# Sample keys and values as one transfer per chunk, Toeplitz matrix and state-space output as one transfer each, U loads and tap stores issued by GpSimd

## The chip, the cores and the metric

The kernel runs on one core of a Trainium2 chip. The metric is the device time of one execution in microseconds. The core has five engines with an instruction stream each: PE (TensorE, matrix products), DVE (VectorE), ACT (ScalarE), POOL (GpSimd) and SP (SyncE), and DMA engines that move data between the chip's memory and the core. A transfer is issued by SP, ACT or POOL and lands later.

## The reference

One inference step of a decoder layer, for a prompt of 1024 tokens and, with the same weights, a sample group of 8 sequences with 4 new tokens each. The mixer runs a dilated attention (8 heads) beside a diagonal state-space model (32 groups of 16 channels, 64 complex states):

```python
q, k, v, u = jnp.split(x @ w_in, [D_ATT, 2 * D_ATT, 3 * D_ATT], axis=-1)
o_att = attend(q, k, v).reshape(Bn, L, D_ATT)
y_ssm, h_re, h_im = s5_mixer(u, h0_re, h0_im, ...)
mixed = jnp.concatenate([rms_norm(o_att, g_att), rms_norm(y_ssm, g_ssm)], axis=-1) @ w_out
x = layer_norm(DEEPNORM_ALPHA * x + mixed, ln1_g, ln1_b)
x = layer_norm(DEEPNORM_ALPHA * x + memory_attention(x, ...), ln2_g, ln2_b)
x = layer_norm(DEEPNORM_ALPHA * x + (jax.nn.silu(x @ w_gate) * (x @ w_up)) @ w_down, ln3_g, ln3_b)

# in s5_mixer, per group: h_t = abar h_(t-1) + bbar u_t, then
y = Re(C h) + D u;  g = gelu(y);  out = g * sigmoid(g @ w_glu + b_glu)
# sample attention: keys and values are [cache of 1024 rows | 4 new rows] of each sequence
```

## The kernel before

The work of interest lies in the first fifth of the execution, in the projection, the state-space part and the sample attention, which are written as interleaved generators.

**Projection.** PE multiplies the weights (split in two parts, `whi` and `wlo`) with the inputs (`a0h`, `a0l`, ...). Lines 209 to 211 give U, the queries and the keys; lines 427 to 429, in gemm_v, give the values. The weights come as `wraw`, loaded by ACT (L180) and split by ACT (L190) and DVE (L191).

**Sample attention.** The eight sequences form two groups (gr) of four batches, and the 1024 cached rows of a sequence form chunks c. For each group and chunk, `load` (L703 to L707) fetches keys ("ckT") or values ("cv") of four batches into tiles called skv. `scores` (L712) multiplies keys with queries; DVE and ACT form the softmax; L772 multiplies the probabilities with the values, chunk by chunk and batch by batch into four strips of one result, L778 adds the new rows, which a small load (L776) puts in a buffer of the same kind, and DVE reads the result in L780. Keys are used while U, queries and keys are projected, values while the values are projected.

**State space.** It runs in two halves (qf) of 16 groups. DVE and POOL build the matrices Bs and CA (L1426 to L1428), U is loaded from `s_u` (L1433), PE transposes Bs (L1437) and ACT copies it into ET (L1439). L1448 forms the taps kp, which are stored to `s_kp` (L1454) and loaded back as a Toeplitz matrix M (L1471). L1466 makes the inputs of the states, HX, DVE and POOL run the chain of steps over them (L1479 to L1500), L1510 and L1514 form Y, and ACT applies the gelu (L1517). The final states go out in L1519, as runs of nine numbers. Y, which lies in a buffer shared with Bs, goes to `s_y` (L1522).

**GLU.** `glu` loads `s_y` back as gT (L494), ACT and DVE split it (L508, L509), and PE multiplies it with weights, between the parts of the prompt's attention (from L594 on), which loads Q, K, Vn and Vf (L564 to L571) on SP.

**Order.** The code says what depends on what; a scheduler then writes each engine's instruction list. Within an engine, instructions start in this order, and an issue that waits holds up all issues behind it. [...]

Of the kernel before, what the change touches and what calls it, by code (L numbers as in the profile page):

```python
# [140 lines left out]
class Body:  # L141
# [121 lines left out]
    def phase12(self, st):  # L263
        tc, nc, a = self.tc, self.nc, self.a
        A = [self.unit("a0"), self.unit("a1")]
        xa = lambda b, k: (A[k // 4][b][0][:, k % 4, :], A[k // 4][b][1][:, k % 4, :])
        scr = lambda name, shape: self.dp.tile(shape, F32, name=name, tag=name)
        self.s_u = scr("s_u", [512, 8 * 144])
        self.s_y = scr("s_y", [512, 8 * 136])
        self.s_kp = scr("s_kp", [2, 16, 16, 240])  # L270
        self.s_q = scr("s_q", [512, 1024])
        self.s_k = scr("s_k", [512, T])
        self.s_v = scr("s_v", [T, 512])
        self.s_mk = scr("s_mk", [128, 2048])
        self.s_mv = scr("s_mv", [128, 2048])
        self.s_z = scr("s_z", [128, 8 * T])
        self.s_x1 = scr("s_x1", [128, 8 * T])
        self.s_h = {(f, b): scr(f"s_h{f}_{b}", [128, 2 * BLK[b][1]]) for f in range(NF // 2) for b in range(3)}
        self.qs = self.t(self.cp, [128, 4, 32], "qs")
        self.ks = self.t(self.cp, [128, 4, 32], "ks")  # L280
        self.os = self.t(self.cp, [128, 4, 32], "os")
        self.qsum = self.t(self.cp, [128, 32], "qsum")
        with tc.tile_pool(name="ostage", bufs=1) as og:
            self.project(A, xa, og)
        self.rest()
# [202 lines left out]
    def glu(self):  # L488
        tc, nc, a = self.tc, self.nc, self.a
        with tc.tile_pool(name="glu", bufs=1) as gp:  # L490
            G, self.mix1 = self.unit("a0"), self.unit("a1")
            gT = self.t(gp, [128, 4, 8, 136], "gT")
            for n in range(4):
                nc.sync.dma_start(gT[:, n].rearrange("p t c -> p (t c)"), self.s_y[n * 128:(n + 1) * 128, :])  # L494
            src = []
# [200 lines left out]
    def sample_attn(self, ap):  # L696
# [6 lines left out]
        def load(src, gr, c):  # L703
            t_ = [self.t(ap, [128, 512], "skv", bufs=8) for _ in range(4)]
            for b4 in range(4):
                nc.sync.dma_start(t_[b4][:], a[src][4 * gr + b4, c])
            return t_  # L707

# [31 lines left out]
    def sample_finish(self, ap, probs, load, scores, masked, tsel, bsel):  # L740
# [15 lines left out]
        for gr, (S, nm, qb) in enumerate(probs):  # L756
# [12 lines left out]
            for c in range(5):  # L769
                vt = load("cv", gr, c)  # L770
                for b4 in range(4):
                    mm(po[32 * b4:32 * b4 + 32, :], PT[:, 128 * c + 32 * b4:128 * c + 32 * b4 + 32], vt[b4][:],  # L772
                       start=c == 0, stop=False)
                yield
            vs = self.t(ap, [128, 512], "skv", bufs=8)
            nc.sync.dma_start(vs[:32], self.s_v[1024:1056, :])  # L776
# [558 lines left out]
    def ssm(self):  # L1335
# [73 lines left out]
        for qf in range(2):  # L1409
# [22 lines left out]
            for i in range(8):  # L1432
                nc.sync.dma_start(U[16 * i:16 * i + 16], su[:, 16 * qf:16 * qf + 16, 7 - i, :])  # L1433
            for q in range(4):
# [18 lines left out]
            for j in range(4):  # L1453
                nc.sync.dma_start(self.s_kp[qf].rearrange("h (q j) x -> h q j x", j=4)[:, :, j, :],  # L1454
                                  kp[32 * j:32 * j + 16].rearrange("p q n h -> p q (n h)"))
# [13 lines left out]
            M = H("ET", (128, 16, 128))  # L1469
            for i in range(8):  # L1470
                g.dma_start(M[16 * i:16 * i + 16], self.s_kp[qf, :, :, 16 * i:16 * i + 128])  # L1471
            X = HX[:, :, :, 9:137].rearrange("p g r (J j) -> p g r J j", j=8)
# [46 lines left out]
            g.dma_start(a["st"][:, gs], HX[:, :, :, 136:145])  # L1519
            sy = self.s_y[:].rearrange("(g h) (t c) -> h g t c", h=16, t=8)  # L1520
            for t_ in range(8):
                nc.sync.dma_start(sy[:, 16 * qf:16 * qf + 16, t_, :], Y[16 * t_:16 * t_ + 16])  # L1522

# [15 lines left out]
```

## Time and profile before

| | |
|---|---|
| median of 3 runs | 1690.15 us (1688.38 to 1690.17) |
| profiled execution | 1694.87 us |
| its span, first to last instruction | 1693.1 us |
| mean granted clock of PE in it | 0.974 |
| busy: PE, DVE, ACT, POOL | 95%, 55%, 35%, 33% |
| bytes moved | 200.71 MB, mean 119 GB/s |

The span is the time from the first to the last instruction, all times in rows are counted from its start. The profiled execution is one more run, taken with the profiler, so its time differs from the median of the others. The granted clock is the share of the full 2.4 GHz that PE got; 0.50 is 1.2 GHz. PEld is PE's loading of weights, which overlaps with its products.

### The profile page before, as it was taken

How to read it: one execution, taken by the hardware profiler on the slowest of the kernel's cores; microseconds unless marked ns; L12 is line 12 of the kernel's file. 1: busy time of each engine (PE TensorE's matmuls, PEld its weight loads, DVE VectorE, ACT ScalarE, POOL GpSimd, SP SyncE). 2: the span in 40 equal slices, each digit the busy share in tenths (PEclk: the TensorE clock that was granted, in tenths of full speed). 3: DMA queues.
4: the chain of work that ended last, by engine and by line, in shares of the span. 5: the costliest groups of instructions: out<-in, count | busy, mean ns of one | idle time of the engine just before them, and what ended most of it. 6: DMA issues, size and time to landing. Idle time of an engine off the chain costs nothing.

```text
span 1693.1 us, 27820 instructions
## 1 busy us (share of the span) xinstructions
PE 1607.1 (95%) x10910; PEld 1468.4 (87%) x10910; DVE 932.8 (55%) x1785; ACT 598.8 (35%) x1164; POOL 558.6 (33%) x568
## 2 busy tenths in 40 slices
PE   7999899899999988999999999999999999999996
PEld 7997765676776977987798989999999999999995
DVE  7655555266544986235537776555555545545545
ACT  5221221266334155235514444333333333211212
POOL 3433413042223545002126555444444441000134
PEclk9998999989999999999999999999999999999998
DMA  7547967613422356226630222222222224422301
GB/s 276 133 101 193 247 169 179 218 61 107 138 74 84 123 193 226 69 75 207 230 115 26 94 70 76 76 76 76 76 76 77 79 77 147 134 76 69 116 38 65
DMA packets 97683, 200.71 MB, mean 119 GB/s; under 512 B 10384, under 2 KB 52880, under 8 KB 96784
## 3 DMA queue, kind: packets, MB, share of 16 engines
q1 hardware_dynamic: 73456, 137.43, 26.0%
q10 hardware_dynamic: 23232, 59.26, 10.8%
q0 software_dynamic: 864, 2.25, 0.9%
q8 instruction: 86, 1.41, 0.3%
q14 instruction: 45, 0.37, 0.1%
HBM read 153.85 MB, written 45.04 MB: 117 GB/s over the span
## 4 chain that ended last, share of the span: by engine, by line
PE 79%; DMA 7%; DVE 6%; issue 2%; ACT 2%; POOL 2%; SPq 1%; POOLq 0%; ACTq 0%; DVEq 0%
PE g L1051 16%; PE g L209 13%; PE g L211 13%; PE g L210 13%; PE s L1051 7%; PE s L594 2%; PE s L596 2%; DMA skv<-in_cv_dram 1%; DMA wraw<-in_wst_dram 1%; PE g L618 1%; DMA skv<-in_ckT_dram 1%; POOL z L855 1%; DVE wlo L191 1%; PE q L772 1%; DMA hr<-s_h 1%
## 5 line engine op out<-in xcount | busy, mean ns | idle before, releaser
L209 PE MATMUL g<-a0h,whi 128*128 128x384 f32 (+1 forms) x768 | 255.4, 334 | 12.6 <-ACT whi L190 9.4
L211 PE MATMUL g<-a0h,wlo 128*128 128x384 f32 (+1 forms) x768 | 251.8, 328 | 3.5 <-DVE wlo L191 3.5
L210 PE MATMUL g<-a0l,whi 128*128 128x384 f32 (+1 forms) x768 | 252.6, 329 | 0.5 <-DVE a0l L509 0.5
L210 PE MATMUL g<-a1l,whi 128*128 128x384 f32 (+1 forms) x672 | 217.7, 324 | 3.8 <-DVE a1l L337 1.8
L209 PE MATMUL g<-a1h,whi 128*128 128x384 f32 (+1 forms) x672 | 220.2, 328 | 0.8 <-ACT a1h L335 0.8
L211 PE MATMUL g<-a1h,wlo 128*128 128x384 f32 (+1 forms) x672 | 217.6, 324 | 0.0
L209 PEld LDWEIGHTS g<-a0h,whi 128*128 128x128 f32 x768 | 147.9, 193 | 19.8 <-ACT whi L190 9.6
L190 ACT CAST whi<-wraw 128x1024 fp32r<-128x1024 f32 x84 | 88.0, 1050 | 186.9 <-PE g L210 103.1
L211 PEld LDWEIGHTS g<-a0h,wlo 128*128 128x128 f32 x768 | 148.0, 193 | 4.8 <-DVE wlo L191 4.3
L210 PEld LDWEIGHTS g<-a0l,whi 128*128 128x128 f32 x768 | 147.9, 193 | 2.0 <-DVE a0l L509 0.7
L191 DVE TENSOR_TENSOR wlo<-wraw,whi 128x1024 fp32r<-128x1024 f32 x84 | 115.7, 1380 | 47.5 <-ACT whi L190 47.3
L209 PEld LDWEIGHTS g<-a1h,whi 128*128 128x128 f32 x672 | 127.5, 190 | 5.7 <-issue 2.8
L210 PEld LDWEIGHTS g<-a1l,whi 128*128 128x128 f32 x672 | 127.4, 190 | 5.2 <-DVE a1l L337 2.0
L211 PEld LDWEIGHTS g<-a1h,wlo 128*128 128x128 f32 x672 | 127.4, 190 | 0.4 <-issue 0.2
L1044 DVE TENSOR_TENSOR wlo<-wt,wlo 128x512 fp32r<-128x512 f32 x100 | 91.9, 920 | 26.2 <-ACT wlo L1043 24.3
L1043 ACT CAST wlo<-wt 128x512 fp32r<-128x512 f32 x100 | 62.0, 620 | 113.3 <-PE g L1051 91.7
L800 DVE TENSOR_TENSOR z<-z,g 128x384 f32<-128x384 f32 (+1 forms) x96 | 49.1, 518 | 88.5 <-PE g L211 88.3
L808 POOL TENSOR_TENSOR acc<-z 128x384 f32<-128x384 f32 (+1 forms) x6 | 8.5, 1416 | 187.3 <-DVE z L800 173.5
L606 POOL TENSOR_SCALAR S<-S,rD 128x128 f32<-128x128 f32 (+7 forms) x64 | 38.4, 607 | 87.7 <-DVE rD L605 54.1
L855 POOL TENSOR_SCALAR z<-z,vneg,vecs 128x384 f32<-128x384 f32 (+1 forms) x36 | 50.5, 1414 | 43.6 <-DVE z L851 43.6
L1219 POOL TENSOR_SCALAR S<-S,rD 128x256 f32<-128x256 f32 x32 | 15.2, 478 | 113.3 <-DVE rD L1208 105.7
L594 PE MATMUL s<-K,Q 64*128 64x256 f32 (+1 forms) x128 | 42.2, 438 | 5.1 <-DVE nm L602 5.1
(459 smaller groups left out, 4031.1 us busy)
## 6 DMA issues: line engine op xcount, KB each, us to landing
wraw<-in_wst_dram ACTq DMA_DIRECT2D x88, 512.0 KB, 4.0
skv<-in_ckT_dram SPq DMA_DIRECT2D x40, 256.0 KB, 5.0
skv<-in_cv_dram SPq DMA_DIRECT2D x40, 256.0 KB, 4.5
wraw<-in_wst_dram SPq DMA_DIRECT2D x20, 512.0 KB, 4.4
wru<-in_wst_dram SPq DMA_DIRECT2D x20, 512.0 KB, 4.2
hr<-s_h SPq DMA_DIRECT2D x22, 384.0 KB, 3.4
kvm<-in_cmk_dram SPq DMA_DIRECT2D x16, 512.0 KB, 4.9
wraw<-in_cmv_dram SPq DMA_DIRECT2D x16, 512.0 KB, 4.3
```

What stands on the lines that cost most here:

```text
L190: self.nc.scalar.copy(h[:], r[:])
L191: self.nc.vector.tensor_tensor(out=l[:], in0=r[:], in1=h[:], op=OP.subtract)
L209: mm(out, wh, xh, start=start, stop=False)
L210: mm(out, wh, xl, start=False, stop=False)
L211: mm(out, wl, xh, start=False, stop=stop)
L594: mm(ps[:, 32 * nf:w], q, k[:, 128 * max(qt - 1, 0):128 * qt + 128], start=True, stop=True)
L606: g.tensor_scalar(out=S[:, :w], in0=S[:, :w], scalar1=rD[:], scalar2=1.0, op0=OP.mult, op1=OP.mult)
L800: self.nc.vector.tensor_tensor(out=z[:, k], in0=z[:, k], in1=ps[:, :n], op=OP.add)
L855: g.tensor_scalar(out=z[:, k], in0=z[:, k], scalar1=sc, scalar2=bi, op0=OP.mult, op1=OP.add)
L1043: act.copy(t_[:, 0], src)
L1044: v.tensor_tensor(out=t_[:, 1], in0=src, in1=t_[:, 0], op=OP.subtract)
L1051: nc.tensor.matmul(ps[:, :n], p_, q_, start=first and k + j == 0, stop=k == 3 and j == 2, skip_group_check=not first)
```

## The change

Four things change. (1) `load` fetches the four batches of a chunk by one transfer of 1 MB into one tile, of which there are two, instead of four transfers of 256 KB into four of eight tiles; eighty issues become twenty. (2) The U loads (8 for each half) and the tap stores (4 for each half) are issued by POOL instead of SP. (3) The Toeplitz matrix of a half is loaded by one transfer, still from POOL, instead of eight. (4) Y is stored by one transfer for each half instead of eight, to an `s_y` whose layout has the half, h, group and t on axes of their own; the four gT loads read from it with an outer dimension of 8. The runs that the transfers consist of keep their lengths. Line numbers shift by at most one: L1471 becomes L1472, L1519 becomes L1520 and L1522 becomes L1521.

```diff
@@ -266,7 +266,7 @@
         xa = lambda b, k: (A[k // 4][b][0][:, k % 4, :], A[k // 4][b][1][:, k % 4, :])
         scr = lambda name, shape: self.dp.tile(shape, F32, name=name, tag=name)
         self.s_u = scr("s_u", [512, 8 * 144])
-        self.s_y = scr("s_y", [512, 8 * 136])
+        self.s_y = scr("s_y", [2, 16, 16, 8 * 136])
         self.s_kp = scr("s_kp", [2, 16, 16, 240])
         self.s_q = scr("s_q", [512, 1024])
         self.s_k = scr("s_k", [512, T])
@@ -491,7 +491,8 @@
             G, self.mix1 = self.unit("a0"), self.unit("a1")
             gT = self.t(gp, [128, 4, 8, 136], "gT")
             for n in range(4):
-                nc.sync.dma_start(gT[:, n].rearrange("p t c -> p (t c)"), self.s_y[n * 128:(n + 1) * 128, :])
+                nc.sync.dma_start(gT[:, n],
+                                  self.s_y[n // 2, :, 8 * (n % 2):8 * (n % 2) + 8, :].rearrange("h g x -> g h x"))
             src = []
             for b in range(3):
                 off, w = BLK[b]
@@ -701,10 +702,9 @@
             nc.sync.dma_start(d[:], s)
 
         def load(src, gr, c):
-            t_ = [self.t(ap, [128, 512], "skv", bufs=8) for _ in range(4)]
-            for b4 in range(4):
-                nc.sync.dma_start(t_[b4][:], a[src][4 * gr + b4, c])
-            return t_
+            t_ = self.t(ap, [128, 4, 512], "skv", bufs=2)
+            nc.sync.dma_start(t_[:], a[src][4 * gr:4 * gr + 4, c].rearrange("b p n -> p b n"))
+            return [t_[:, b4] for b4 in range(4)]
 
         def scores(o, n, q, keys):
             for hp in range(4):
@@ -769,10 +769,10 @@
             for c in range(5):
                 vt = load("cv", gr, c)
                 for b4 in range(4):
-                    mm(po[32 * b4:32 * b4 + 32, :], PT[:, 128 * c + 32 * b4:128 * c + 32 * b4 + 32], vt[b4][:],
+                    mm(po[32 * b4:32 * b4 + 32, :], PT[:, 128 * c + 32 * b4:128 * c + 32 * b4 + 32], vt[b4],
                        start=c == 0, stop=False)
                 yield
-            vs = self.t(ap, [128, 512], "skv", bufs=8)
+            vs = self.t(ap, [128, 512], "skv", bufs=2)
             nc.sync.dma_start(vs[:32], self.s_v[1024:1056, :])
             for b4 in range(4):
                 mm(po[32 * b4:32 * b4 + 32, :], PT[:32, 640 + 32 * b4:672 + 32 * b4], vs[:32], start=False, stop=True)
@@ -1430,7 +1430,7 @@
             ET, U = H("ET", (128, 8, 2, 128)), H("U", (128, 16, 144))
             su = self.s_u[:].rearrange("(g h) (s c) -> h g s c", h=16, s=8)
             for i in range(8):
-                nc.sync.dma_start(U[16 * i:16 * i + 16], su[:, 16 * qf:16 * qf + 16, 7 - i, :])
+                g.dma_start(U[16 * i:16 * i + 16], su[:, 16 * qf:16 * qf + 16, 7 - i, :])
             for q in range(4):
                 ps = self.ps2()
                 for j in range(4):
@@ -1451,7 +1451,7 @@
             act.copy(kp[:, :, 7:15, :].rearrange("p q n h -> p q (n h)"), ps[:, :512].rearrange("p (q x) -> p q x", q=4))
             v.tensor_tensor(out=kp[:, :, 7, :], in0=kp[:, :, 7, :], in1=dd[:, 4 * qf:4 * qf + 4, :], op=OP.add)
             for j in range(4):
-                nc.sync.dma_start(self.s_kp[qf].rearrange("h (q j) x -> h q j x", j=4)[:, :, j, :],
+                g.dma_start(self.s_kp[qf].rearrange("h (q j) x -> h q j x", j=4)[:, :, j, :],
                                   kp[32 * j:32 * j + 16].rearrange("p q n h -> p q (n h)"))
             yield
 
@@ -1467,8 +1467,9 @@
                            U[:, 2 * gl + z, 8:144], start=True, stop=True)
                 act.copy(HX[:, gl, :, 9:145], ps[:, 0:272].rearrange("p (r c) -> p r c", r=2))
             M = H("ET", (128, 16, 128))
-            for i in range(8):
-                g.dma_start(M[16 * i:16 * i + 16], self.s_kp[qf, :, :, 16 * i:16 * i + 128])
+            taps = self.s_kp[qf]
+            taps = bass.AP(taps.tensor, taps.offset, [[16, 8], *[list(x) for x in taps.ap[:2]], [1, 128]])
+            g.dma_start(M[:], taps)
             X = HX[:, :, :, 9:137].rearrange("p g r (J j) -> p g r J j", j=8)
             qa = lambda e_: e_[:, gs].unsqueeze(2)
             m1, m2 = S("w1", (128, 8, 2, 16)), S("w2", (128, 8, 2, 16))
@@ -1517,9 +1518,7 @@
                     act.activation(Y[:].rearrange("p (g z) c -> p z g c", z=2)[:, z, g0:g0 + cnt, :],
                                    pz[z][:, :136 * cnt].rearrange("p (g c) -> p g c", c=136), AF.Gelu_apprx_tanh)
             g.dma_start(a["st"][:, gs], HX[:, :, :, 136:145])
-            sy = self.s_y[:].rearrange("(g h) (t c) -> h g t c", h=16, t=8)
-            for t_ in range(8):
-                nc.sync.dma_start(sy[:, 16 * qf:16 * qf + 16, t_, :], Y[16 * t_:16 * t_ + 16])
+            nc.sync.dma_start(self.s_y[qf].rearrange("h g (t c) -> t (h g) c", t=8), Y[:])
 
 
 
```

First the order on SP, around the store of the first half's Y. Before, the key tile of chunk 2 of the second group (skv_2069 is its last) is followed by U loads, the eight s_y stores and then chunk 3, whose first tile is skv_2126:

```order
L706 DMA skv_2069<-in_ckT_dram 128x512
L1433 DMA U_2214<-s_u 16x16x144 x3
L1522 DMA s_y<-Bs_1775 16x16x136 x8
L1433 DMA U_2214<-s_u 16x16x144
L706 DMA skv_2126<-in_ckT_dram 128x512
```

In the changed kernel the same place reads as follows; skv_1956 to skv_2120 are chunks 1 to 4 of the second group, and skv_2646 is the first value chunk:

```order
L706 DMA skv_1956<-in_ckT_dram 128x4x512
L706 DMA skv_2010<-in_ckT_dram 128x4x512
L1521 DMA s_y<-Bs_1738 8x256x136
L706 DMA skv_2064<-in_ckT_dram 128x4x512
L706 DMA skv_2120<-in_ckT_dram 128x4x512
L706 DMA skv_2646<-in_cv_dram 128x4x512
```

The U loads have left SP; the store of Y still stands between chunks 2 and 3, as one issue. On SP behind the second half's Y, before and then after:

```order
L1522 DMA s_y<-Bs_3052 16x16x136 x8
L494 DMA gT_3445<-s_y 128x1088 x2
L558 DMA mask_3175<-in_mask_p_dram 128x448
L564 DMA Q_3177<-s_q 128x1024
L564 DMA K_3178<-s_k 128x1024
L569 DMA Vn_3425<-s_v 128x8x128
L571 DMA Vf_3426<-s_v 128x4x128 x2
L494 DMA gT_3445<-s_y 128x1088 x2
```

```order
L1521 DMA s_y<-Bs_2917 8x256x136
L494 DMA gT_3297<-s_y 128x1x1088 x2
L559 DMA mask_3027<-in_mask_p_dram 128x448
L565 DMA Q_3029<-s_q 128x1024
L565 DMA K_3030<-s_k 128x1024
L570 DMA Vn_3277<-s_v 128x8x128
L572 DMA Vf_3278<-s_v 128x4x128 x2
L494 DMA gT_3297<-s_y 128x1x1088 x2
```

One issue of s_y stands there instead of eight, and all that follows keeps its order. On PE, the value products (L772) of chunk 2 of the first group stand as follows before; skv_2809 to skv_2812 are the four batches, and L427 to L429 belong to the projection of the values:

```order
L429 MATMUL g_2780<-whi_2120,a1l_15_84 128x256
L772 MATMUL q_2726<-skv_2809,qb_2714 32x512
L772 MATMUL q_2726<-skv_2810,qb_2714 32x512
L427 MATMUL g_2821<-whi_2060,a0h_8_77 128x256
L428 MATMUL g_2821<-wlo_2061,a0h_8_77 128x256
L429 MATMUL g_2821<-whi_2060,a0l_9_78 128x256
L427 MATMUL g_2821<-whi_2060,a0h_8_77 128x256
L428 MATMUL g_2821<-wlo_2061,a0h_8_77 128x256
L772 MATMUL q_2726<-skv_2811,qb_2714 32x512
L429 MATMUL g_2821<-whi_2060,a0l_9_78 128x256
L427 MATMUL g_2821<-whi_2060,a0h_8_77 128x256
L428 MATMUL g_2821<-wlo_2061,a0h_8_77 128x256
```

The third batch stands five projection matmuls behind the second, the fourth comes five further on. The batches of chunks 3 and 4 of that group and of chunks 2 and 3 of the other stand apart in the same way. In the changed kernel, all four batches of every chunk stand together, here those of chunk 2 (skv_2716), as one row with x4:

```order
L427 MATMUL g_2722<-whi_2004,a0h_8_77 128x256
L428 MATMUL g_2722<-wlo_2005,a0h_8_77 128x256
L429 MATMUL g_2722<-whi_2004,a0l_9_78 128x256
L772 MATMUL q_2645<-skv_2716,qb_2633 32x512 x4
L427 MATMUL g_2722<-whi_2004,a0h_8_77 128x256
L428 MATMUL g_2722<-wlo_2005,a0h_8_77 128x256
L429 MATMUL g_2722<-whi_2004,a0l_9_78 128x256
```

Between chunk 1's and chunk 2's products stand 33 projection matmuls there; behind the last sample product (L784) and ahead of the GLU stand 92 where there were about 81. On POOL, the eight U loads of the second half stand between the products L1426, L1427 and the first L1428 of that half, ahead of L1460 and L1461; before, SP issued them.

## Rows read from the trace of the kernel before

**Rows 1.** Page, busy us of each engine (share of the span)

```profile
PE 1607.1 (95%) x10910; PEld 1468.4 (87%) x10910; DVE 932.8 (55%) x1785; ACT 598.8 (35%) x1164; POOL 558.6 (33%) x568
```

**Rows 2.** All waits of PE, 120 to 345 us: total us, times, longest

```profile
PE q L712 <- DMA skv<-in_ckT_dram: 5.6, 5, 4.1
PE q L772 <- DMA skv<-in_cv_dram: 5.4, 3, 2.9
PE s L1437 <- ACT ET L1439: 4.4, 1, 4.4
PE s L594 <- DVE nm L602: 2.7, 2, 2.3
PE g L209 <- ACT a0h L508: 2.5, 2, 1.3
```

**Rows 3.** Stretches: length, busy PE, PEld, DVE, ACT, POOL, PEclk, DMA share, GB/s

```profile
150.80:164.40 13.60, 12.01 (x71) 10.02 (x72) 0.46 (x3) 2.19 (x3) 0.50 (x1) 0.50 0.59 192
...
176.00:188.00 12.00, 12.00 (x131) 11.19 (x130) 1.05 (x4) 2.39 (x6) 0.96 (x3) 1.00 1.13 246
...
205.40:212.20 6.80, 5.98 (x26) 5.59 (x27) 5.55 (x11) 3.63 (x9) 2.83 (x4) 0.50 0.90 308
...
290.00:298.00 8.00, 5.14 (x16) 2.21 (x15) 0.00 (x0) 0.32 (x1) 0.00 (x0) 0.79 0.81 189
...
335.00:348.70 13.70, 12.39 (x62) 9.30 (x62) 6.62 (x19) 7.90 (x18) 1.65 (x4) 0.50 0.60 207
```

**Rows 4.** Chain that ended last, around 139 us: start, us, what

```profile
138.30 0.22 SPq L706
...
139.61 12.73 DMA skv<-in_ckT_dram
152.39 1.92 PE q L712 x26
```

**Rows 5.** Timeline of POOL, issues and one wait

```profile
138.47 1.22 POOL L1519 DMA_DIRECT2D out_dram<-HX  x1 [0.63 <-DVE HX L1483]
...
187.19 0.74 POOL L1428 TENSOR_TENSOR Bs<-p,p 128x256 f32<-128x256 f32 x1 [10.96 <-DMA U<-s_u]
...
232.94 4.48 POOL L1471 DMA_DIRECT2D ET<-s_kp  x8 [10.97 <-PE s L1466]
```

**Rows 6.** Line L1519 (state store), issue to landing

```profile
DMA to landing us min/median/max: 13.7/14.2/14.7
```

**Rows 7.** Line L706 (key and value loads), issue to landing

```profile
DMA to landing us min/median/max: 2.5/4.9/13.7
```

**Rows 8.** Timeline of SP, its DMA issues

```profile
176.54 6.14 SPq L1522 DMA_DIRECT2D s_y<-Bs  x8
...
184.14 3.00 SPq L706 DMA_DIRECT2D skv<-in_ckT_dram  x4
...
234.90 15.16 SPq L706 DMA_DIRECT2D skv<-in_cv_dram  x12
...
309.95 6.40 SPq L1522 DMA_DIRECT2D s_y<-Bs  x8
```

**Rows 9.** Chain through the PV products: start, us, what

```profile
233.89 0.99 PE q L772 x8
...
236.28 11.47 DMA skv<-in_cv_dram
...
248.85 0.32 PE g L428
...
254.24 0.97 PE q L772 x2
...
305.80 0.12 PE g L429
```

**Rows 10.** Timeline of DVE, first PV result of a group

```profile
266.89 0.69 DVE L780 TENSOR_TENSOR sS<-q,sm 128x512 f32<-128x512 f32 x1 [9.98 <-PE q L778]
```

**Rows 11.** Chain from the second Y to glu: start, us, what

```profile
316.52 7.48 DMA gT<-s_y
```

## The prediction, made before the changed kernel was run

> **What bounds the kernel now.** I read the page first: PE is busy for 1607.1 us of the span, 95% [rows 1]. A change to transfers can therefore only win where PE waits or runs at the lower clock, or where PE itself gets fewer or shorter instructions. The lines that the change touches all lie before about 345 us, so I next listed all waits of PE between 120 and 345 us: 5.6 us in L712 for keys, 5.4 us in L772 for values, 4.4 us in L1437 for a copy of ACT, and 2.7 and 2.5 us in the attention and GLU matmuls that follow the second state-space half. These five rows add up to 20.6 us [rows 2]. Then the stretches: the granted clock is half (1.2 instead of 2.4 GHz) in 150.8 to 164.4, 205.4 to 212.2 and 335 to 348.7 us, and in part of 290 to 298 us, each right behind one of these waits [rows 3]. PE is busy for 12.01, 5.98 and 12.39 us there; at the full clock the same work would take half, so the clock costs some 6.0, 3.0 and 6.2 us, and in the fourth stretch, of 8 us with a mean clock of 0.79, at most 1.7. That is 17 us more. About 38 us in all is what better transfers could reach.
>
> **Part one: the last key chunk of the first batch group.** Four loads of 256 KB now go out one behind another from 138.30 us, the fourth at 139.61. It lands 12.73 us later and L712 resumes only at 152.39 [rows 4]; the wait is the longest one of that row, 4.1 us. It is slow because of what POOL issues at 138.47 us, the state store of L1519 with its runs of nine numbers [rows 5], which takes 13.7 to 14.7 us to land [rows 6]; loads usually take 4.9 us, with 2.5 and 13.7 as the ends [rows 7]. The one transfer of 1 MB would go out whole at 138.30, ahead of the store. PE needs it at 148.3 (152.39 less 4.1), 10.0 us later. So it is in time unless it too takes over 10 us. In time, the 4.1 us wait and the 6.0 us of half clock behind it vanish: 10 us. Caught behind the store after all: nothing. The price has no row of its own, so the ends are 0 and 10; I take 10, since the transfer starts before the store and the usual landing is half the slack.
>
> **Part two: the first s_y store and the second half's matrices.** SP issues eight s_y stores for 6.14 us from 176.54; only then, at 184.14, do the four loads of the next key chunk follow [rows 8]. The four short waits that they cause (the 5.6 us of L712 less 4.1) are 1.5 us. In the new order this chunk still stands behind s_y, but behind one issue, not behind eight and a U load, so it starts some 5 us earlier and they go. POOL's (and DVE's) matrices for the second half overwrite the buffer that s_y is read from, and start at 187.19 us [rows 5], 10.7 us behind Y's end; the row names a U load as the last to land; it stands behind s_y on SP. One transfer of 128x16x136 numbers of four bytes, 1.11 MB, takes 4.5 us at the 246 GB/s that 176 to 188 us shows [rows 3], and 9.0 us at half that; with the 2.5 us that the shortest load took [rows 7] it lands 7 to 11.5 us behind Y. The start moves by -3.7 to +0.8 us. Behind it stand the 4.4 us wait of L1437 and 3.0 us of half clock. [...] Ends: -8.9 (all 1.5 + 4.4 + 3.0) and +2 (waits as they are, the start later, less the 1.5). I take -4, the 1.5 and a third of the rest.
>
> **Part three: the value products.** Three chunks of the first group and two of the second now have their four batches singly between projection matmuls: twenty singles by the order of PE, at 0.97 us each, where four batches together take 0.99 [rows 9]. Grouped, the 20 singles become 5 groups: 20 x 0.97 - 5 x 0.99 = 14.5 us less of PE. The first projection matmul behind each takes 0.32 instead of 0.12 us [rows 9]; 15 fewer such switches are 3.0 us more. Against this, PE must now wait for all four. With two buffers, chunk 2's load goes out when the first group of products ends, 234.90 us as before [rows 8]. The nearest row is the load that took 11.47 us while the Toeplitz matrix, issued from 232.94, was in flight [rows 5, 9]; PE gets to chunk 2 some 33 projection matmuls behind chunk 1, whose group ends about 237.6: 33 x 0.12 = 4 us more [rows 9], so at 241.6. Landing at 246.4, it stalls PE by 5 us, and I add 3.0 us of half clock as behind the like wait of 4.4 us. In exchange the present waits of 5.4 us and the 1.7 us of clock may go. Ends: -24.6 (all of 14.5, 3.0, 5.4, 1.7) and 0 (both groups stall like this, 16 us, and the order of the step chain takes back the rest). DVE stands 9.98 us at the first group's result, with the step chain of the second half queued behind it [rows 10]; that result comes earlier as the products get shorter, but the store of L1519 then starts earlier too and meets the value loads of the second group. For that I take only half of the gain: (14.5 + 3.0 + 1.7 - 5 - 3.0) / 2, and the present waits as kept: -6.
>
> **Part four: the second s_y store, gT and GLU.** Here Y's end to the first gT is the path: eight stores from 309.95 for 6.40 us, gT at 316.52, landed 7.48 us later at 324.00, 14.05 us behind Y [rows 8, 11]. In the new order SP issues s_y at once and two gT loads directly behind it. They move 1.11 and twice 0.56 MB: 2.2 MB, 9.0 us at 246 GB/s, 18 us at half of that, with 2.5 us ahead: 11.5 to 20.5 us. So -2.6 to +6.5 us, and at the bad end the clock behind it loses some 3 us more. PE has eleven more projection matmuls to cover it, 1.3 us. I take +3, since s_y, gT and the eight other loads of this stretch now start closer together.
>
> [...]
>
> **Edits costed at nothing.** Sixteen U loads and eight s_kp stores on POOL: a POOL issue takes 0.56 us (4.48 over eight [rows 5]), so 4.5 us for the second half's U, ahead of POOL's first matrix. The 10.96 us that POOL stands idle there cover them; without that cover they would put 4.5 us on part two. The single Toeplitz issue frees 3.9 us of POOL, which nobody waits for.
>
> **Sum.** -10 - 4 - 6 + 3 = -17 us against the profiled execution of 1694.87 us, whose span is 1693.1. That execution lies 4.7 us above the median of the runs, 1690.15; the difference is taken over: 1690.15 - 17 = 1673 us.
>
> **The rivals.** *First, full-rate transfers* (chance 0.22): all four parts go near their good ends, -10 - 7 - 8 - 1 = -26, 1664 us. For it speaks that the eight small stores take as long to issue as the data needs; against it, that 240 to 300 us still has 1 MB waits. *Second, the chunk is caught by the store again* (0.20): part one is 0, and the values' stalls eat part three down to -2: 0 - 4 - 2 + 3 = -3, 1687 us; that would be about no change. For it speaks that the fourth load was overtaken by a store issued 1.1 us ahead of it; the new one leads by 0.2 us. *Third, the other side: s_y and gT at half rate* (0.18). Place: Y to matrices, and Y to GLU. If the eight-fold outer dimension confines them, and the key and value loads beside them share these engines, s_y at 176 us lands 11.5 + 4.5 = 16 us behind Y and the matrices start 5 us later than before, the step chain with them, and Y to GLU grows by 6.5 + 3 of clock + 4.5 for the shared engines = 14 in place of 3: -10 + 5 - 6 + 14 = +3, and with part one lost too, +13; I put it at 1696 us. It decides from where the two places together cost 17 us more than I take for them. The forecast itself has 0.40 and, alone, 1667 to 1680 us.
>
> Within 0.2% (3.4 us, about what a measurement of this kernel can tell from no change) lie most of the second rival's cases and the edge of the third. So faster 0.68, same 0.13, slower 0.19. The range 1660 to 1693 leaves out the bulk of the third rival and little else.
>
> **What would show it.** Part one: no wait of L712 at 148 us and full clock behind it. Part two: the second half's first L1428 within 11.5 us of Y's end, L1437 without its 4.4 us. Part three: L772 in groups of eight records near 1.0 us, one wait of some 5 us at chunk 2. Part four: gT landing 11.5 to 20.5 us behind Y. The prediction is wrong if L712 still waits at 148 us, if s_y takes over 12 us, or if L772 waits for more than 12 us in all.

## The result and the profile after

The changed kernel takes 1704.55 us (median of 4 runs, 1701.2 to 1709.48), the kernel before 1689.27 in the same comparison. The ratio that the comparison estimates is 1.0083, with a 95% interval of 1.0055 to 1.011 (the two medians alone give 1.0090). It is 15 us slower, where 17 us less was predicted, and lies outside the range. The profiled execution of the changed kernel has a span of 1702.5 us, 9.4 more than that of the kernel before, whose own profiled run lay above its median.

PE is busy for less time. The page's line of engines, as [rows 1] of before:

```profile
PE 1587.5 (93%) x10910; PEld 1463.3 (86%) x10910; DVE 935.6 (55%) x1785; ACT 598.2 (35%) x1164; POOL 562.3 (33%) x578
```

That is 19.6 us less than before; the value products (L772) alone are busy for 12.6 us instead of 26.9. The waits of PE between 120 and 360 us (total us, times, longest) answer to [rows 2]:

```profile
PE g L209 <- ACT a0h L509: 11.2, 1, 11.2
PE s L1437 <- ACT ET L1439: 9.2, 1, 9.2
PE q L712 <- DMA skv<-in_ckT_dram: 8.0, 1, 8.0
PE q L772 <- DVE HX L1483: 8.0, 1, 8.0
PE g L619 <- POOL S L607: 7.7, 1, 7.7
PE q L772 <- DMA skv<-in_cv_dram: 6.0, 2, 5.2
PE s L595 <- DVE nm L603: 1.9, 1, 1.9
```

They add up to 52.0 us. Before, the five rows of [rows 2] came to 20.6; the same view has three more, for 0.9, 0.5 and 0.4 us, which make it 22.4. So 29.6 us more waiting stands against 19.6 us less work: 10.0 us, about the 9.4 of the spans. The work did shrink as the grouping of value products promised; what was lost was lost in waits. The timeline of SP, as in [rows 8], shows the two places where much of it begins:

```profile
166.19 0.75 SPq L1521 DMA_DIRECT2D s_y<-Bs  x1
170.88 11.68 SPq L706 DMA_DIRECT2D skv<-in_ckT_dram  x2
...
308.23 0.64 SPq L1521 DMA_DIRECT2D s_y<-Bs  x1
309.71 9.67 SPq L494 DMA_DIRECT2D gT<-s_y  x2
```

SP issues s_y in 0.75 us instead of 6.14. But the two key loads behind it occupy SP for 11.68 us, and the two gT loads behind the second s_y for 9.67 us. The line of the key loads in the view by line (issues; duration in ns, min/median/max) says that one issue did it:

```profile
L706 SPq DMA_DIRECT2D skv<-in_ckT_dram x10: 367/368/10303, 17.6 to 181.3; - x10
...
DMA to landing us min/median/max: 5.0/6.8/19.3
```

One issue took 10303 ns where 368 is usual (the one at 170.88 us, the first behind s_y), and the slowest landing that the trace has of these loads is 19.3 us. The timeline of POOL, as in [rows 5], has the matrices of the second half:

```profile
165.08 4.47 POOL L1433 DMA_DIRECT2D U<-s_u  x8 [14.20 <-PE s L1511]
...
185.85 0.97 POOL L1428 TENSOR_TENSOR Bs<-p,p 128x256 f32<-128x256 f32 x1 [15.93 <-DMA s_y<-Bs]
```

They start 19.66 us behind the issue of s_y (185.85 less 166.19); before it was 10.7 us behind Y. The row names s_y itself as what came last. The U loads, 4.47 us of POOL for eight, lie wholly ahead of that wait.

Three places in the timeline of PE, and one in that of ACT, answer to the other parts:

```profile
147.53 1.08 PE L712 MATMUL q<-skv,qb 128*32 128x128 f32 x32
...
256.17 1.94 PE L772 MATMUL q<-skv,qb 128*32 128x512 f32 x8 [7.99 <-DVE HX L1483]
...
330.75 1.01 PE L209 MATMUL g<-a0h,whi 128*128 128x384 f32 x2 [11.20 <-ACT a0h L509]
```

```profile
329.82 3.33 ACT L509 CAST a0h<-gT 128x384 fp32r<-128x384 f32 x4 [15.56 <-DMA mask<-in_mask_p_dram]
```

At 147.53 us the first group's last key chunk starts without a wait. At 256.17 the first group's value chunk 3 (counted from 0, as the prediction counts) has waited 7.99 us; its releaser is named as DVE, but its load, issued at 236.73, is the one that took 19.3 us. Chunk 2, for which the prediction had a wait of 5 us, came at 240.83 without one. (The expectations below call the later chunk "value chunk 2", in both groups; counted from 0 it is chunk 3.) At 329.82 ACT begins to split gT, 21.6 us behind Y's end, and at 330.75 the first GLU product starts, 22.5 us behind it and after 11.20 us of waiting; before it came 15.1 us behind. The stretches, with the columns of [rows 3], show what the clock did:

```profile
148.00:160.00 12.00, 12.00 (x116) 10.35 (x108) 2.26 (x7) 2.19 (x3) 2.81 (x5) 1.00 0.93 225
...
182.38:192.62 10.24, 4.28 (x42) 3.80 (x43) 6.60 (x10) 0.00 (x0) 6.38 (x8) 0.50 0.76 257
199.44:209.68 10.24, 5.14 (x22) 5.14 (x23) 10.07 (x17) 3.00 (x6) 6.33 (x8) 0.50 0.52 160
250.64:260.88 10.24, 4.71 (x21) 3.08 (x22) 5.43 (x40) 0.37 (x1) 0.00 (x0) 0.50 0.60 185
291.60:301.84 10.24, 9.55 (x48) 6.14 (x52) 0.00 (x0) 0.34 (x1) 0.00 (x0) 0.50 0.31 103
322.32:335.98 13.66, 5.23 (x18) 4.16 (x20) 4.91 (x7) 6.16 (x11) 0.00 (x0) 0.50 0.98 266
339.39:353.04 13.65, 6.00 (x31) 4.40 (x32) 1.97 (x8) 5.23 (x13) 1.68 (x4) 0.50 0.82 249
```

Behind 148 us the clock is full now. Half clock stands behind each long wait, and PE is busy for 34.9 us in these six stretches. In the last but one, PE's 128x384 products start 320 ns apart; at 145 us, at full clock, they start 174 ns apart. With half taken for the work at full clock, an estimate, the clock costs 17.5 us, about the 17 of before, though at other places.

### The profile page after: what moved, and what is told of

It is laid out like the page before. It is cut to its first block, busy times and chain, and to the rows that moved or that the text cites. A ratio compares the mean times of both kernels' runs of the same rounds, so it can differ in the third digit from the quotient of the medians.

```text
span 1702.5 us, 27642 instructions
## 1 busy us (share of the span) xinstructions
PE 1587.5 (93%) x10910; PEld 1463.3 (86%) x10910; DVE 935.6 (55%) x1785; ACT 598.2 (35%) x1164; POOL 562.3 (33%) x578
## 5 line engine op out<-in xcount | busy, mean ns | idle before, releaser
L209 PE MATMUL g<-a0h,whi 128*128 128x384 f32 (+1 forms) x768 | 254.0, 332 | 21.5 <-ACT a0h L509 11.2
L209 PE MATMUL g<-a1h,whi 128*128 128x384 f32 (+1 forms) x672 | 221.3, 330 | 0.9 <-ACT a1h L335 0.9
L209 PEld LDWEIGHTS g<-a0h,whi 128*128 128x128 f32 x768 | 146.9, 192 | 28.4 <-ACT a0h L509 11.8
L209 PEld LDWEIGHTS g<-a1h,whi 128*128 128x128 f32 x672 | 128.1, 191 | 6.3 <-issue 3.1
L1041 POOL TENSOR_TENSOR wt<-wraw,wraw 128x512 f32<-128x512 f32 x30 | 39.4, 1313 | 22.1 <-DVE wlo L1044 22.1
```

The costliest lines, as they stand in the source:

```text
L209: mm(out, wh, xh, start=start, stop=False)
L1041: g.tensor_tensor(out=src, in0=q[p_], in1=q[q_], op=op)
```

## The experiments

**Theories.** A: the outer dimension of 8 in the new s_y store and gT loads is what makes them slow, as fewer DMA engines carry them (the outer dimension is the slowest axis of an access pattern; the old stores and gT loads have 16 or more). B: one large issue with many runs is slow whatever its shape. C: the loss sits in the 1 MB loads and the transfers on GpSimd. D: the transfers on GpSimd cost something. E: the Toeplitz load has the same fault as s_y. All times are medians; each comparison also ran the kernel before, and ratios are to that. Each trace is one execution, and some lie 5 to 10 us off their kernel's median. The runs of one kernel lay 4 to 23 us apart, those of the kernel before too (1680 to 1695 us in the first comparison), so that differences of 2 to 4 us between two kernels are not resolved, even where their traces differ.

### e1: the same bytes with 128 as the outer dimension

```diff
-        self.s_y = scr("s_y", [2, 16, 16, 8 * 136])
+        self.s_y = scr("s_y", [2, 16, 128, 136])
...
-            nc.sync.dma_start(self.s_y[qf].rearrange("h g (t c) -> t (h g) c", t=8), Y[:])
+            nc.sync.dma_start(self.s_y[qf].rearrange("g p c -> p g c"), Y[:])
```

The gT loads read rows of 1088 numbers of this s_y, 128 in each. 

> The changed kernel, with the same bytes of Y stored in runs of the same 544 B and read back in rows of the same 4352 B, but with 128 rows as the outer dimension of the s_y store and the gT loads instead of 8. Y then lies in another order in s_y, so the GLU reads permuted channels; the work is the same. If the outer dimension of 8 is what makes s_y and gT slow (theory A): s_y lands within 9 us of its issue instead of 18.8, gT within 12, the key load behind s_y is issued at once instead of taking 10.3 us, the wait of 8.0 us in L712 and most of the 9.2 us in L1437 and 11.2 us in L209 go, and the time falls to about 1675 us. If the slowness comes from the number of runs behind one issue (theory B): s_y still takes over 15 us and the time stays near 1704. If the loss sits in the 1 MB loads and the transfers on GpSimd (theory C): s_y gets faster, but the time stays above 1695.

(The 18.8 us are from the issue to the last of Y's packets; the start of POOL above is the time that matters.) Measured: 1687.10 us, ratio 0.9994 (0.9965 to 1.0024): 17 us below the changed kernel. The issues of s_y, by SP's timeline, and how long s_y and gT took to land (us, min/median/max, first s_y, then gT):

```profile
172.66 0.37 SPq L1522 DMA_DIRECT2D s_y<-Bs  x1
177.35 4.77 SPq L707 DMA_DIRECT2D skv<-in_ckT_dram  x2
...
309.16 0.37 SPq L1522 DMA_DIRECT2D s_y<-Bs  x1
310.65 1.63 SPq L494 DMA_DIRECT2D gT<-s_y  x2
```

```profile
DMA to landing us min/median/max: 6.3/10.0/13.8
```

```profile
DMA to landing us min/median/max: 6.6/7.1/8.0
```

In the second half, s_y lands in 6.3 us and gT within 8.0, and the two gT issues take 1.63 us instead of 9.67. In the first half, where U loads and key loads run beside it, s_y still takes 13.8 us, not the 9 expected, and POOL's matrices start 13.9 us behind it. Of the waits of PE, the one for the key load behind s_y falls from 8.0 to 2.9 us and the 11.2 us in L209 goes, but one that was expected to go stays:

```profile
PE s L1438 <- ACT ET L1440: 8.9, 1, 8.9
```

Theory B falls: one issue with the same 2048 runs landed in 6.3 us in the second half when its outer dimension was 128. A holds for most of the loss: 17 us, as much as the change lost. But the time comes only to that of before, not to the 1675 us expected, so something else takes what parts one and three should give.

### e2, e3 and e4: one part undone, one part alone

e2 is the changed kernel with s_y, its store and the gT loads as before. e3 is the kernel before with only `load` and its two buffers changed. e4 is the kernel before with only s_y changed. The edits, each from the diff of the change, in their first lines:

```diff
# e2, on the changed kernel
-            nc.sync.dma_start(self.s_y[qf].rearrange("h g (t c) -> t (h g) c", t=8), Y[:])
+            for t_ in range(8):
+                nc.sync.dma_start(sy[:, 16 * qf:16 * qf + 16, t_, :], Y[16 * t_:16 * t_ + 16])
# e3, on the kernel before
-            t_ = [self.t(ap, [128, 512], "skv", bufs=8) for _ in range(4)]
+            t_ = self.t(ap, [128, 4, 512], "skv", bufs=2)
# e4, on the kernel before
-                nc.sync.dma_start(sy[:, 16 * qf:16 * qf + 16, t_, :], Y[16 * t_:16 * t_ + 16])
+            nc.sync.dma_start(self.s_y[qf].rearrange("h g (t c) -> t (h g) c", t=8), Y[:])
```

> The changed kernel with only the s_y store and gT loads as before (eight stores for each half). Theories A and B: about 1680 us, as the single store is what costs; C: above 1695 us.

> The kernel before with only the keys and values as one 1 MB transfer per chunk. Theories A and B: the gains of parts one and three of the prediction alone, 10 to 16 us faster than before, 1674 to 1680 us. C: as slow as before or slower, 1690 to 1700 us.

> The kernel before with only the single s_y store and its gT loads. Theories A and B: slower by 15 to 25 us, 1705 to 1715 us; C: within 5 us of before.

| | median us | ratio to before (95%) |
|---|---|---|
| e2, s_y as before | 1686.74 | 1.0002 (0.9976 to 1.0027) |
| e3, 1 MB loads alone | 1680.38 | 0.996 (0.9936 to 0.9984) |
| e4, s_y alone | 1708.12 | 1.0122 (1.0085 to 1.0159) |

e4 is 20 us slower than the kernel before: the s_y part alone costs more than the whole change. e3 is 8 us faster, a little short of the 10 to 16 us that A gave it: theory C falls as the main cause. e2, expected at 1680 us by A, is as fast as the kernel before and some 6 us slower than e3, from which it differs by the Toeplitz load and the GpSimd issues (the two intervals just overlap). The waits of PE in e3, the longest rows:

```profile
PE q L771 <- DMA skv<-in_cv_dram: 9.2, 3, 4.2
PE q L711 <- DMA skv<-in_ckT_dram: 5.1, 2, 2.9
PE g L209 <- ACT a0h L508: 3.7, 2, 2.0
PE s L1436 <- ACT ET L1438: 3.3, 1, 3.3
```

They are shorter than in the changed kernel at each place, but the values' 9.2 us are above the 5.4 of before: the new wait for whole chunks that part three reckoned with.

### e8: an outer dimension of 4

e4 with Y stored by two issues for each half, each of them four of the eight rows t:

```diff
+            sv = self.s_y[qf].rearrange("h g (t c) -> t (h g) c", t=8)
+            for t_ in range(0, 8, 4):
+                nc.sync.dma_start(sv[t_:t_ + 4], Y[16 * t_:16 * t_ + 64])
```

> The kernel before with s_y stored by two issues for each half, whose outer dimension is 4, and the gT loads of the changed kernel. If the outer dimension sets how many engines carry a transfer (theory A): the two stores together take about twice as long as the single one of e4 (18.8 us from issue to landing in the first half, 16.5 us from first to last packet), 30 us or more, and the time rises to 1720 to 1735 us. If a single large issue is what costs (theory B): two smaller issues are no slower than the one of e4, 1700 to 1710 us.

Measured: 1726.48 us, ratio 1.0218 (1.0179 to 1.0257), 37 us above before, 18 above e4. (In e4 POOL's matrices start 14.55 us behind the issue; the 18.8 us of the expectation were taken from the changed kernel's end of packets, and the 16.5 us are not e4's: there the packets of this store span 10.5 us.) The clearest sight of the cause is in the stretches behind the second half's Y, where nearly nothing but s_y and then gT runs; the last two columns are the busy share of the DMA engines and GB/s. First before (eight stores), then e1 (outer dimension 128), e4 (8), e8 (4):

```profile
314.00:318.00 4.00, 4.00 (x36) 4.00 (x35) 0.00 (x0) 0.37 (x1) 0.00 (x0) 1.00 0.89 214
```

```profile
312.00:316.00 4.00, 4.00 (x36) 4.00 (x35) 0.00 (x0) 0.69 (x2) 0.00 (x0) 1.00 0.99 268
```

```profile
313.00:321.00 8.00, 8.00 (x68) 8.00 (x69) 0.23 (x1) 0.97 (x3) 0.68 (x3) 1.00 0.47 112
```

```profile
320.00:328.00 8.00, 8.00 (x69) 8.00 (x68) 0.00 (x0) 0.97 (x3) 0.69 (x3) 1.00 0.30 78
```

The share goes 0.89, 0.99, 0.47, 0.30, and the rate 214, 268, 112, 78 GB/s: read as engines, which these rows don't list singly, that is about half of them for 8, and for 4, with some other traffic beside it, a little over a quarter. In the first half SP issues s_y, and POOL's matrices start, by their timelines in e4 and then e8:

```profile
172.16 0.72 SPq L1521 DMA_DIRECT2D s_y<-Bs  x1
...
186.71 0.97 POOL L1429 TENSOR_TENSOR Bs<-p,p 128x256 f32<-128x256 f32 x1 [14.87 <-DMA s_y<-Bs]
```

```profile
170.44 9.46 SPq L1523 DMA_DIRECT2D s_y<-Bs  x2
...
192.25 0.87 POOL L1429 TENSOR_TENSOR Bs<-p,p 128x256 f32<-128x256 f32 x1 [22.12 <-DMA s_y<-Bs]
```

So the matrices start 14.55 us behind the issue in e4 and 21.8 in e8. That is 1.5 times as long, and the packets of this store span 17.4 us instead of 10.5: longer, as A has it, but not the 30 us that it gave. The time is where A put it: the price nearly doubles, from 20 to 37 us, and B does not give that. So A is shown for these transfers with outer dimensions of 8 and 4, against 128; how the share goes with other dimensions isn't shown.

### e6, e7 and e12: the Toeplitz load

e6 is e3 with the single Toeplitz load; e12 is the same on e10 (below). e7 is e1 with the Toeplitz source laid out as 128 rows of the same runs, so that M holds other rows of the taps:

```diff
-            taps = bass.AP(taps.tensor, taps.offset, [[16, 8], *[list(x) for x in taps.ap[:2]], [1, 128]])
+            taps = bass.AP(taps.tensor, taps.offset, [[448, 128], [240, 16], [1, 128]])
```

> The kernel before with the 1 MB key and value loads and the single Toeplitz load. If the single Toeplitz load, whose source has an outer dimension of 8, is the second cause (theory E): the wait at the first group's value chunk 2 is 8 us instead of the 3.8 of e3, half clock follows it for some 10 us, the Toeplitz load takes over 20 us to land in the second half, and the time is 6 to 10 us above e3, 1686 to 1692 us. If it is not: as e3, 1676 to 1684 us.

> e1 with the Toeplitz load also given 128 rows as its outer dimension, same bytes and same runs of 512 B, so that M holds other rows of the stored taps and Y other values; the work is the same. If the outer dimension of 8 makes the Toeplitz load slow: it lands within 12 us instead of 22.7, the wait at value chunk 2 falls from 8.6 to 4 us or less, and the time falls below e1, to 1676 to 1682 us. If POOL's large packets are slow by themselves: it lands after 20 us again and the time stays as e1's, 1687.

> e10 with the single Toeplitz load of the changed kernel. With the state store out of the way, the price of that load alone. If its outer dimension of 8 costs time (theory E): it lands after 20 us in the second half, the wait at the first group's value chunk 2 is 8 us, half clock follows, and the time is 6 to 10 us above e10, 1672 to 1676 us. If the wait is hidden or given back later: within 3 us of e10.

Measured: e6 1680.61 us (ratio 0.9968, 0.9935 to 1.0002), e7 1682.34 (0.9954, 0.9926 to 0.9982), e12 1667.59 (0.9864, 0.9842 to 0.9887). (e1 and e7 compute other results, as their expectations say; their transfers keep their sizes and runs.) How long the Toeplitz load took to land (us, min/median/max) in e6, and then in e1 and e7, which differ by it alone:

```profile
DMA to landing us min/median/max: 15.8/19.2/22.5
```

```profile
DMA to landing us min/median/max: 13.7/18.2/22.7
```

```profile
DMA to landing us min/median/max: 6.9/8.5/10.1
```

And value chunk 3 of the first group in the timelines of PE, e1 and then e7:

```profile
256.65 1.94 PE L773 MATMUL q<-skv,qb 128*32 128x512 f32 x8 [8.61 <-DMA skv<-in_cv_dram]
```

```profile
249.98 1.06 PE L773 MATMUL q<-skv,qb 128*32 128x512 f32 x8
```

The second-half Toeplitz load goes from 22.7 to 10.1 us, the load of chunk 3 beside it from 20.0 to 9.5, and the wait of 8.61 us for that chunk is gone, against a new one of 1.87 us at chunk 2: theory E holds for the mechanism, and on a transfer that POOL issues. (e7 also reads the taps in another order of rows; that this plays no part isn't shown.) Its price in the total is not settled. e7 is 4.8 us below e1 by the medians, e12 1.9 above e10 and e6 0.2 above e3, all within what the runs resolve; the 6 to 10 us that E gave e6 and e12 did not come. In e6 and e12 the wait is there again (8.6 and 7.7 us in L771). In the one profile of e12 the second Y ends at 284.95 us, by the first s_y issue, in that of e10 at 280.96: 4 us of it are still there. Whether the rest of the kernel gives them back isn't shown.

### e5 and e11: U loads and tap stores on GpSimd

```diff
-                nc.sync.dma_start(U[16 * i:16 * i + 16], su[:, 16 * qf:16 * qf + 16, 7 - i, :])
+                g.dma_start(U[16 * i:16 * i + 16], su[:, 16 * qf:16 * qf + 16, 7 - i, :])
...
-                nc.sync.dma_start(self.s_kp[qf].rearrange("h (q j) x -> h q j x", j=4)[:, :, j, :],
+                g.dma_start(self.s_kp[qf].rearrange("h (q j) x -> h q j x", j=4)[:, :, j, :],
```

> The kernel before with the 1 MB key and value loads and with the U loads and tap stores on GpSimd; s_y and the Toeplitz matrix as before. If the U loads and tap stores on GpSimd are free, as the prediction has it: as e3, 1676 to 1684 us. If they are a second cause (theory D): 1688 to 1695 us, with a longer wait of L712 at the second group's chunk 3 and the second half's transposes.

> e10 with the U loads and tap stores on GpSimd too. If these are free: within 3 us of e10. If they cost, by the software transfers' larger share of the DMA engines beside the first s_y store: 3 to 6 us above e10, with s_y landing later than in e10 in the first half.

e5, e3 with these issues on GpSimd, takes 1682.92 us (0.998, 0.9954 to 1.0007), 2.5 above e3; e11, the same on e10, 1669.72 (0.9882, 0.9854 to 0.991), 4.1 above e10. Both intervals overlap those of their partners: theory D's cost of 2 to 4 us is likely, and not shown; the 1688 to 1695 us that it gave e5 did not come. The landing of s_y (us, min/median/max) in e3 and then e5 points the same way:

```profile
DMA to landing us min/median/max: 2.8/5.1/6.4
```

```profile
DMA to landing us min/median/max: 2.8/5.4/10.7
```

With SP as their issuer, four U loads go out ahead of the first half's s_y and four behind it; on GpSimd all eight go out beside its first five stores (166.82 to 170.73 us, s_y from 167.93), and the slowest s_y store lands after 10.7 instead of 6.4 us.

### e9 and e10: the state store in long runs

```diff
-            g.dma_start(a["st"][:, gs], HX[:, :, :, 136:145])
+            sc = H("sc", (128, 8, 2, 9))
+            act.copy(sc[:], HX[:, :, :, 136:145])
+            g.dma_start(a["st"][:, gs], sc[:])
```

> The kernel before, with the final states first copied by ACT into a contiguous tile of 144 numbers per partition and stored from there, so that the state store is 128 runs of 576 B instead of 2048 runs of 36 B. If the state store is what held the fourth load of the first group's last key chunk (part one of the prediction): the store lands within 5 us instead of 14, the 4.1 us wait of L712 at 148 us goes and the clock stays full behind it, and the time falls by 6 to 10 us, 1679 to 1683 us. If that load was slow for another reason: the wait stays, and the time is within 3 us of before.

> e3 (1 MB key and value loads only) with the same contiguous state store. If the state store still catches 1 MB loads: the wait at the first group's last key chunk (2.2 us in e3) and the one at the second group's value chunk 2 (4.2 us in e3) go, and the time is 4 to 10 us below e3, 1670 to 1676 us. If the 1 MB loads wait for their own size: both waits stay and the time is as e3, 1678 to 1683 us.

e9, on the kernel before, takes 1679.19 us (0.9934, 0.9907 to 0.996), 10.7 us less. The state store's landing, against [rows 6], and the first group's last key chunk in the timeline of PE, against [rows 4]:

```profile
DMA to landing us min/median/max: 3.8/4.6/5.4
```

```profile
145.62 1.08 PE L712 MATMUL q<-skv,qb 128*32 128x128 f32 x32
```

The store lands in 3.8 to 5.4 us instead of 13.7 to 14.7, and the wait before L712 is gone. So part one of the prediction named the right cause. Its 10 us is not measured alone: the copy serves both halves, and the 2.9 us wait for the second group's values behind the second state store ([rows 2], the longest of L772) is gone, too. e10, on e3, takes 1665.67 us (0.9854, 0.9827 to 0.9881), 24 us below the kernel before and 15 below e3; it beats both kernels, and lies further below e3 than the 4 to 10 us that were expected. The two waits that stood behind the state stores in e3, 2.2 us at the first group's last key chunk and 4.2 at the second group's value chunk 3, are gone but for 0.4 us at the latter. What is left in L711 and L771 is 3.7 us for the key chunk behind s_y and 4.1 us for the first group's value chunk 3 (put down to DVE, though its load lands just ahead):

```profile
PE q L771 <- DVE HX L1482: 4.1, 1, 4.1
PE q L711 <- DMA skv<-in_ckT_dram: 3.7, 1, 3.7
...
PE q L771 <- DMA skv<-in_cv_dram: 1.8, 3, 1.0
```

## Why the prediction was wrong, step by step

The mechanism that decided was the third rival, s_y and gT at half rate, which had a chance of 0.18 and an estimate of 1696 us. It was right in its place and even in its sign, and too cheap. Of the prediction's three signs of being wrong two came true: s_y took over 12 us, and L772 waited for 14.0 us in all; L712 did not wait at 148 us. The step that failed is the landing of s_y and gT, taken near the full rate, in the terms of -4 and +3 us, together with a wait that the prediction did not have, that of SP's next issue.

**Part one, -10 us: right, by luck.** In the changed kernel's profile the chunk starts without a wait and the clock behind it is full: its load landed 9.8 us after its issue, at 147.49 us, 0.04 us before PE took the chunk. But in e1, which issues the same loads in the same order, L713 waited again:

```profile
151.46 1.94 PE L713 MATMUL q<-skv,qb 128*32 128x128 f32 x32 [5.74 <-DMA skv<-in_ckT_dram]
```

All the other traces with the 1 MB loads and the old state store have this wait: 4.8 us in e2, 2.2 in e3, 2.5 in e5, 4.3 in e6, 6.2 in e7. The load's small lead does not decide it, either: it goes out 0.28 us ahead of the store in the changed kernel and 0.29 in e1, where it took 15.4 us to land. What decides is not shown. So the second rival, for which the prediction had 0.20, is the usual case, and it is part of why e1 and e2 came only to the time of before. With the copy of e10 to e12 the wait is gone in all three traces. The cure is not a larger load but a store without runs of 36 B.

**Part two, -4 us: the step that failed first.** The prediction set the sum nearer to the full rate of s_y than to the half. (Its other end of +2 us does not come out of its terms either: 0.8 us later less 1.5 is -0.7.) The matrices started 19.66 us behind the issue. The half rate was the right end (e4: a DMA share of 0.47, 112 GB/s), but even that end missed two things. The other transfers of the stretch are in it: U and key loads stand beside s_y (13.8 us in e1's first half, 6.3 in its second). And SP's next issue was held for 10.3 us, which the prediction didn't have at all: the key load behind s_y went out late, and L712 got an 8.0 us wait in place of the 1.5 us that were to vanish. Those 1.5 us were not to be had in any case: with the 1 MB loads this chunk still waits 2.9 us with the fast store of e1 and with the eight stores of e3. The other 2.5 us of the -4, a third of L1437's wait and of the half clock behind it, were the author's estimate, and no run shows them. L1437 waited 9.2 instead of 4.4 us, but not for s_y's rate: the wait is 8.9 us in e1 and e7, too, whose store is fast, and e4, with the slow store alone, has none there. It ends with a copy on ACT, as the prediction said; why it grew stays open.

**Part three, -6 us: right in its kind, short on both sides.** PE's busy time fell by 19.6 us, where 17.5 was worked out (14.5 of products, measured as 14.3, and 3.0 of switches). The wait came one chunk later than predicted, at chunk 3, and was 8.0 us and not 5, as that load took 19.3 us and not the 11.47 of the nearest row. In e3, with eight Toeplitz loads, the 1 MB load took 14.4 us, so some 3 us come with the 1 MB loads; the other 5 come with the single Toeplitz load, which the prediction costed at nothing (19.9 in e6 as well). Both landed together: the Toeplitz load at 255.03 us, the values at 256.03. At the second group's chunk 3 another 5.2 us came, behind the second state store. e3, where the Toeplitz load is as before, keeps a net 8 us of parts one and three.

**Part four, +3 us: the other large miss.** ACT could split gT only 21.6 us behind Y, just past the bad end of 20.5 us for its landing, and the first GLU product came 7.4 us later than before: the bad end, +6.5 us and the clock behind it, was the right one, and the sum took +3. L209 waited 11.2 us, and L619 7.7 us, for a softmax step that ACT began only after 10.2 us of idle time, put down to a weight load; what held that load isn't shown. In the kernel before both rows together were below 4 us. e4, with the slow s_y and gT alone, has 7.8 and 9.5 us there, e1 with the fast ones none and 3.9.

**Edits costed at nothing.** The issues on POOL were covered, as said, by the wait for s_y; what they may cost is the company they give to s_y, 2 to 4 us. The Toeplitz load was not free: the slowest landing went from 10.7 us for one of the eight to 21.9.

Added up from the experiments: -8 us for the 1 MB loads (e3), 17 to 20 us for s_y and gT (e1 and e2 against the changed kernel, e4 against before), 2 to 4 us for POOL, and 0 to 5 us for the Toeplitz load: 11 to 21 us, around the 15 measured. These prices come from different kernels and need not add up. The error was one of weighing. The diff and the order showed the outer dimension of 8 plainly, and the third rival named it; that it would halve the rate of s_y and gT was the author's estimate, which no row of before shows, and it was put at 0.18. The runs showed a DMA share of 0.47 in e4 and of 0.30 in e8, where e1 had 0.99.

## What to carry to other kernels

Before several transfers are joined into one, look at the outer dimension that the joined access pattern has on either side: eight transfers of 16 rows each ran at a DMA share of 0.89 and 214 GB/s (before), one of 8 x 256 runs at 0.47 and 112 GB/s (e4), and behind such a store in the changed kernel SP's next issue of a key load took 10.3 us instead of 0.37. A transfer of many tiny runs, here 2048 of 36 B, is worth a small copy into a contiguous tile, since it can delay what is in flight beside it: here that copy gave 10.7 us alone (e9) and 24 us together with the 1 MB loads (e10). And a load of a whole chunk can be as late as its slowest companion: value chunk 3 landed 1.0 us behind the Toeplitz load in the changed kernel, and e1's last key chunk together with the state store (151.42 and 151.49 us). Its landing is better bounded by the slowest transfer that will share its time than by a usual landing.

## What was not expected of the hardware

SP's issue of a 1 MB load took 10303 ns instead of 368 behind the s_y store with an outer dimension of 8; the first gT issue behind the second store took 7172 ns, and in e4 7.43 us. Issues behind the 128-row store of e1 showed nothing of the kind (0.37 us for the key load, 1.63 instead of 9.67 us for SP's two gT issues). A transfer that POOL issues was slow with an outer dimension of 8, too: the Toeplitz load landed in 22.7 us (e1), with 128 in 10.1 us (e7); how many engines carried it isn't shown. And 2048 runs of 36 B, 74 KB in all, took 14 us to land, and a 1 MB load issued 0.29 us ahead of them on another queue took 15.4 us (e1), where the same bytes in 128 runs landed in 3.8 to 5.4 us (e9) and 5.3 to 5.8 us (e10), and the load in 5.6 (e10).
